# High and low part of the moving tiles as two blocks, each at its own distance from the weights

## The chip, the cores and the metric

The kernel runs on one core of one Trainium2 chip. The metric is the device time of one execution in microseconds, as the median of several runs.

## What is computed

Two layers of a hybrid trunk, run for two groups of 128 tokens each (a context group and a denoising group) that share all weights; the model is 2048 wide, the MLP 8192. Cut to what matters:

```python
def run(x, cond, s_init, latent):
    cond_act = silu(cond)
    for layer in range(2):
        sh1, sc1, g1, sh2, sc2, g2 = split(cond_act @ w_ada[layer] + b_ada[layer], 6)
        h = rms_norm(x, norm_g[layer, 0]) * (1 + sc1) + sh1
        m = hyena(h, ...) if layer == 0 else retention(h, ...)   # projections in, mixer, projection out
        x = x + g1 * m
        h = rms_norm(x, norm_g[layer, 1]) * (1 + sc2) + sh2
        x = x + g2 * (square(relu(h @ w1[layer])) @ w2[layer])
    return rms_norm(x, final_g)
```

The Hyena mixer has an input projection to 3 x 2048 and an output projection; the retention mixer has projections q and k (2048 each), v and g (4096 each) and `w_o` from 4096 back to 2048. All is float32.

## The kernel before

The activations are held transposed, features on the 128 partitions and the 256 tokens of both groups along the free axis. To reach float32 accuracy with the one-pass float32r matmul, each weight tile and each activation tile is split in a high part (the value rounded to float32r) and a low part (the rest), and a product is three matmuls: weight high by activation high (L348), weight high by activation low (L349), weight low by activation high (L350), all into one PSUM tile of 256 columns. The weight part is the operand that is loaded into the array (128 columns), the activation part is the moving one (256 columns). `gemm` (L357) runs over output tiles of 128 features and steps of 8 feature tiles, so one step is 24 matmuls; `next_w` hands it a pair `wh`, `wl` of 128 x 1024 that ScalarE (L293, high) and VectorE (L296, low) made from a weight tile that SyncE's DMA queue brought. For v and g, `gemm_v` (L428) turns the roles round: the activation part is loaded and the weight part moves, 512 columns (L440 to L442).

All instructions stand in an order written out by hand; the adaLN products are woven into it, most of them on VectorE (L254), some on TensorE (L241, groups of 16 matmul records with 256 columns), a few per stage.

Stages in order of time, with their number of 256-column matmuls and the moving tile: Hyena input projection (2304, `ht0`), Hyena output projection (768, `zt`), MLP 0 (3072 on `ht1` for w1 and 3072 on `ut` for w2, in four rounds that alternate), retention (per head 192 for q and k on `ht2`, 192 of 512 columns for v and g; 1536 and 1536 in all; 1536 on `yt` for `w_o` in four groups), MLP 1 (3072 on `ht3`, 3072 on `ut`).

Where the tiles lie: every `wh` and `wl` buffer is 4096 bytes per partition and all start at the same residue modulo 256 bytes, and a weight tile of 128 columns is 512 bytes, so every weight load starts at that one residue. `SHIFT` (L72) gives for each moving tile its distance from the weights modulo 256 bytes: 192 for all, 0 for `ht2`. A moving tile is 128 x 2 x 512 elements: for each of two feature tiles 256 high elements and then 256 low ones, 1024 bytes each, so high and low parts have the same distance. The tiles of pool `h` (`ht0` to `ht3` and part of `yt`) are 1088 elements and are used from an offset (`slid`, L83); the pools `u` (`zt`, `ut`, the rest of `yt`) begin at distance 192 (`U_BASE`). `norm_tiles` (L530) writes `ht`, `split_to` (L576) writes `ut`, `fin` (L945) `zt` and `ytr` (L1212) `yt`: each time a high part on ScalarE and a low part on VectorE. `WIDE` (L26) is empty, so what it would switch on never runs.

Of the kernel before, what the change touches and what calls it, by code (L numbers as in the profile page):

```python
# [10 lines left out]
F32 = mybir.dt.float32  # L11
# [6 lines left out]
P = 128  # L18
# [7 lines left out]
WIDE = ()  # L26
# [5 lines left out]
U_BASE = 192  # L32
# [66 lines left out]
def hybrid_trunk_kernel(ctx: ExitStack, tc, a):  # L99
# [241 lines left out]
    def products(acc, w, x, first, last):  # L341

        wh, wl = w
        if acc.shape[-1] == 512:
            T.matmul(acc, wh, x, start=first, stop=False)
            T.matmul(acc[:, 0:256], wl, x[:, 0:256], start=False, stop=last)
            return
# [9 lines left out]
    def gemm(act, n_half, evacs, mid=None, first=None, clear=None, lead=LEAD, wide=False):  # L357
# [7 lines left out]
        def open_acc(t):  # L365
            opens.setdefault(t, True)
            if first is None or t >= FIRST:
                accs[t] = pacc.tile([P, 512 if wide else 256], F32, tag="acc", name="acc")
# [146 lines left out]
    def norm_mod(l, h, pool):  # L515
# [12 lines left out]
        return (lambda k: tiles[k // 2][:, k % 2, :]), mid  # L528

    def norm_tiles(l, h, rstd, nt, seq, tiles, small=False):  # L530


        def scale(i):
            t = nt.tile([P, 2, 256], F32, tag="nt", name="nt") if small else \
                nt.tile([P, 2, 512], F32, tag="u", name="nt")[:, :, 0:256]
# [840 lines left out]
```

## Time and profile before

| | |
|---|---|
| median of 3 runs | 2872.66 us (2871.03 to 2876.06) |
| the profiled execution | 2874.03 us |
| its span, first to last instruction | 2872.3 us |
| mean granted clock of TensorE | 0.986 |
| busy: PE, PEld, DVE, ACT | 98%, 91%, 71%, 48% |
| DMA, mean | 244 GB/s |

PE is TensorE's matmul, PEld its weight load, DVE VectorE, ACT ScalarE. A matmul's shown duration (276 to 284 ns for 256 columns) is longer than the distance from one start to the next (113 to 120 ns), since matmuls are pipelined. To get that distance, starts have to be compared, or counts in a stretch of known length.

### The profile page before, as it was taken

To read this page: it belongs to the slowest core of one execution; us is meant where nothing else is said; L and a number is where in the kernel's file an instruction comes from. 1 tells how busy PE (TensorE), PEld (TensorE's weight loads), DVE (VectorE), ACT (ScalarE), POOL (GpSimd) and SP (SyncE) were. 2 spreads that over 40 slices of the span, in tenths; PEclk is the share of its full clock that TensorE was granted. 3 is DMA by queue.
4 is the path that set the end of the run, shared out by engine and by line. 5 is a ranking of instruction groups with operands and counts; after the bars stand their busy time and mean duration, and the time that the engine had idled before them with its cause. 6 is when DMAs were issued, how large, how long until landed. Compare 5 with 4: busy or idle time off the path is not lost.

```text
span 2872.3 us, 52521 instructions
## 1 busy us (share of the span) xinstructions
PE 2806.4 (98%) x22182; PEld 2625.6 (91%) x22182; DVE 2052.0 (71%) x2587; ACT 1389.9 (48%) x1960; POOL 24.7 (1%) x57
## 2 busy tenths in 40 slices
PE   7999999999999999999999999999999999999998
PEld 3689899989999999998888988988889999999998
DVE  3589999767777777786766887888774555555656
ACT  3454543465453443546545445454455445354554
POOL 1000000000000000000000000000000000000000
PEclk8999999999999999999999999999999999999999
DMA  9867776677676676666766676777665555565652
GB/s 368 322 245 282 269 286 246 246 267 273 245 265 242 244 268 241 253 242 243 251 246 224 232 278 246 256 264 281 239 234 206 201 206 200 197 224 213 224 192 103
DMA packets 105650, 701.03 MB, mean 244 GB/s; under 512 B 12115, under 2 KB 12308, under 8 KB 25796
## 3 DMA queue, kind: packets, MB, share of 16 engines
q1 hardware_dynamic: 95698, 672.58, 65.3%
q0 software_dynamic: 4384, 15.51, 1.5%
q10 hardware_dynamic: 5330, 9.57, 0.9%
q8 instruction: 174, 2.85, 0.4%
q14 instruction: 64, 0.52, 0.0%
HBM read 687.13 MB, written 10.49 MB: 243 GB/s over the span
## 4 chain that ended last, share of the span: by engine, by line
PE 86%; issue 5%; DVE 5%; DMA 3%; ACT 1%; POOL 0%; POOLq 0%; ACTq 0%; DVEq 0%
PE acc L348 23%; PE acc L349 23%; PE acc L350 23%; PE accv L440 3%; PE accv L442 3%; PE accv L441 3%; PE ada_ps L241 1%; DVE junk L254 1%; DVE wl L296 1%; DMA raw<-w_ada 1%; PE y_ps L1185 1%; ACT wh L293 1%; DMA st<-state 1%; DMA xT<-x 1%; PE y_ps L940 0%
## 5 line engine op out<-in xcount | busy, mean ns | idle before, releaser
L296 DVE TENSOR_TENSOR wl<-raw,wh 128x1024 fp32r<-128x1024 f32 x896 | 1092.6, 1224 | 666.0 <-ACT wh L293 664.6
L293 ACT CAST wh<-raw 128x1024 fp32r<-128x1024 f32 x896 | 940.2, 1053 | 1093.6 <-PE acc L349 842.6
L348 PE MATMUL acc<-ht,wh 128*128 128x256 f32 x3328 | 944.7, 284 | 6.2 <-ACT wh L293 6.2
L350 PE MATMUL acc<-ht,wl 128*128 128x256 f32 x3328 | 937.4, 282 | 6.1 <-DVE wl L296 6.1
L349 PE MATMUL acc<-ht,wh 128*128 128x256 f32 x3328 | 936.2, 281 | 0.6 <-DVE ht L560 0.6
L348 PEld LDWEIGHTS acc<-ht,wh 128*128 128x128 f32 x3328 | 634.5, 191 | 20.4 <-issue 9.4
L350 PEld LDWEIGHTS acc<-ht,wl 128*128 128x128 f32 x3328 | 636.8, 191 | 8.1 <-DVE wl L296 8.0
L349 PEld LDWEIGHTS acc<-ht,wh 128*128 128x128 f32 x3328 | 633.1, 190 | 2.8 <-issue 1.2
L348 PE MATMUL acc<-ut,wh 128*128 128x256 f32 x2048 | 572.6, 280 | 0.0
L350 PE MATMUL acc<-ut,wl 128*128 128x256 f32 x2048 | 572.5, 280 | 0.0
L349 PE MATMUL acc<-ut,wh 128*128 128x256 f32 x2048 | 572.4, 279 | 0.0
L254 DVE CUSTOM_DVE_ANT_0 junk<-raw,cb 128x2048 bf16<-128x2048 f32 x224 | 511.6, 2284 | 0.0
L350 PEld LDWEIGHTS acc<-ut,wl 128*128 128x128 f32 x2048 | 388.3, 190 | 0.1
L348 PEld LDWEIGHTS acc<-ut,wh 128*128 128x128 f32 x2048 | 386.6, 189 | 0.8 <-issue 0.8
L349 PEld LDWEIGHTS acc<-ut,wh 128*128 128x128 f32 x2048 | 384.4, 188 | 0.0
L440 PE MATMUL accv<-wh,ht 128*128 128x512 f32 x512 | 204.7, 400 | 0.0
L442 PE MATMUL accv<-wh,ht 128*128 128x512 f32 x512 | 200.1, 391 | 0.0
L441 PE MATMUL accv<-wl,ht 128*128 128x512 f32 x512 | 199.4, 389 | 0.0
L348 PE MATMUL acc<-yt,wh 128*128 128x256 f32 x512 | 143.4, 280 | 0.0
L349 PE MATMUL acc<-yt,wh 128*128 128x256 f32 x512 | 141.7, 277 | 0.0
L350 PE MATMUL acc<-yt,wl 128*128 128x256 f32 x512 | 141.6, 277 | 0.0
L440 PEld LDWEIGHTS accv<-wh,ht 128*128 128x128 f32 x512 | 96.2, 188 | 21.5 <-ACT wh L293 1.4
(213 smaller groups left out, 2480.5 us busy)
## 6 DMA issues: line engine op xcount, KB each, us to landing
raw<-w SPq DMA_DIRECT2D x250, 1024.0 KB, 5.0
raw<-w_ada SPq DMA_DIRECT2D x192, 1024.0 KB, 6.4
raw<-w_qkvg SPq DMA_DIRECT2D x93, 1024.0 KB, 5.5
raw<-hy_w_in SPq DMA_DIRECT2D x42, 1024.0 KB, 5.8
raw<-w_o SPq DMA_DIRECT2D x32, 1024.0 KB, 5.0
raw<-hy_w_out SPq DMA_DIRECT2D x12, 1024.0 KB, 6.7
st<-state POOLq DMA_DIRECT2D x16, 512.0 KB, 4.2
new_state<-so ACTq DMA_DIRECT2D x32, 256.0 KB, 4.6
```

The source lines that it names most:

```text
L241: T.matmul(st_["ps"][32 * c:32 * c + 32, :], cpad[:, 2 * u[4] + k, :], w[:, k, 256 * c:256 * c + 256], start=not started and k == 0, stop= ...
L254: V.tensor_tensor_reduce(out=junk, in0=raws[u[1:5]], in1=cb[:, r], scale=1.0, scalar=0.0, op0=ALU.mult, op1=ALU.add, accum_out=st_["acc"][ ...
L293: S.copy(whf, src)
L296: V.tensor_tensor(out=wl.rearrange("p k c -> p (k c)"), in0=src, in1=whf.bitcast(F32), op=ALU.subtract)
L348: T.matmul(acc, wh, x[:, 0:256], start=first, stop=False)
L349: T.matmul(acc, wh, x[:, 256:512], start=False, stop=False)
L350: T.matmul(acc, wl, x[:, 0:256], start=False, stop=last)
L440: T.matmul(accs[r], hi, wh[:, k, :], start=first, stop=False)
L441: T.matmul(accs[r], hi, wl[:, k, :], start=False, stop=False)
L442: T.matmul(accs[r], lo, wh[:, k, :], start=False, stop=last)
L1185: T.matmul(s["y", 1], s["qd"][:, d, q, :], s["state", d][:, q, :], start=False, stop=(d == 1 and q == 1))
```

## The change

High and low part of a moving tile become two blocks of 512 elements, one behind the other (each holding two feature tiles of 256), and the low block can be pushed away from the high one by up to 64 elements. `SHIFT` now holds a pair for each stage: the high block's distance from the weights in bytes modulo 256, and how much further the low block lies.

| tile | high, low before | high, low after |
|---|---|---|
| `ht0` | 192, 192 | 192, 224 |
| `zt` (`hy_u`) | 192, 192 | 192, 192 |
| `ht1` | 192, 192 | 192, 0 |
| `ut` in MLP 0 | 192, 192 | 96, 192 |
| `ht2` | 0, 0 | 192, 192 |
| `yt` | 192, 192 | 192, 192 |
| `ht3` | 192, 192 | 32, 64 |
| `ut` in MLP 1 | 192, 192 | 224, 224 |

`slid` returns the two blocks as a pair of access patterns; `k_of` picks feature tile k of both, and `products`, `gemm_v` and the writers take the pair in place of column ranges of one tile. The `u` tiles of the MLPs become 1088 elements (9 per pool), those of `hy_u` and `ret_u` stay at 1024. `shifted` and all that hangs on `WIDE` are removed. The diff, cut to its core:

```diff
-SHIFT = {"ht0": 192, "ht1": 192, "ht2": 0, "ht3": 192, "yt": 192, "hy_u": 192, "mlp_u0": 192, "ret_u": 192, "mlp_u1": 192}
...
-def slid(pool, name):
-
-    o = SHIFT[name] // 4
-    t = pool.tile([P, 1088], F32R, tag="h", name=name)
-    return t[:, o:o + 1024].rearrange("p (a b) -> p a b", a=2)
+SHIFT = {"ht0": (192, 32), "ht1": (192, 64), "ht2": (192, 0), "ht3": (32, 32), "yt": (192, 0),
+         "hy_u": (192, 0), "mlp_u0": (96, 96), "ret_u": (192, 0), "mlp_u1": (224, 0)}
+
+
+def slid(pool, tag, name, at, n=1088):
+
+    a, b = SHIFT[at]
+    a, b = (a - (U_BASE if tag == "u" else 0)) % 256 // 4, b // 4
+    t = pool.tile([P, n], F32R, tag=tag, name=name)
+    return tuple(t[:, o:o + 512].rearrange("p (k c) -> p k c", k=2) for o in (a, a + 512 + b))
+
+
+def k_of(tiles, k):
+    return tuple(t[:, k % 2, :] for t in tiles[k // 2])
...
         wh, wl = w
-        if acc.shape[-1] == 512:
...
-        T.matmul(acc, wh, x[:, 0:256], start=first, stop=False)
-        T.matmul(acc, wh, x[:, 256:512], start=False, stop=False)
-        T.matmul(acc, wl, x[:, 0:256], start=False, stop=last)
+        hi, lo = x
+        T.matmul(acc, wh, hi, start=first, stop=False)
+        T.matmul(acc, wh, lo, start=False, stop=False)
+        T.matmul(acc, wl, hi, start=False, stop=last)
...
-                    hi, lo = (x[:, o + r * 128:o + (r + 1) * 128] for o in (0, 256))
+                    hi, lo = (part[:, r * 128:(r + 1) * 128] for part in x)
...
-            ht = slid(hp, ("ht0", "ht1", "ht2", "ht3")[2 * l + h])
-            S.copy(ht[:, :, 0:256], slots[i][0])
+            ht = slid(hp, "h", "ht", f"ht{2 * l + h}")
+            S.copy(ht[0], slots[i][0])
...
-            V.tensor_tensor(out=ht[:, :, 256:512], in0=h32, in1=ht[:, :, 0:256].bitcast(F32), op=ALU.subtract)
+            V.tensor_tensor(out=ht[1], in0=h32, in1=ht[0].bitcast(F32), op=ALU.subtract)
...
-        S.copy(dst[:, 0:256], src)
-        return lambda: V.tensor_tensor(out=dst[:, 256:512], in0=src, in1=dst[:, 0:256].bitcast(F32), op=ALU.subtract)
+        S.copy(dst[0], src)
+        return lambda: V.tensor_tensor(out=dst[1], in0=src, in1=dst[0].bitcast(F32), op=ALU.subtract)
...
-                        us[j // 2] = up.tile([P, 2, 512], F32R, tag="u", name="ut")
+                        us[j // 2] = slid(up, "u", "ut", f"mlp_u{l}")
...
-            yt = slid(hp, "yt") if h == 7 else \
-                up.tile([P, 2, 512], F32R, tag="u", name="yt")
+            yt = slid(hp, "h", "yt", "yt") if h == 7 else slid(up, "u", "yt", "ret_u", 1024)
```

## Rows read from the trace of the kernel before

**Rows 1.** The page: engines, granted clock in 40 slices, chain that ended last.

```profile
PE 2806.4 (98%) x22182; PEld 2625.6 (91%) x22182; DVE 2052.0 (71%) x2587; ACT 1389.9 (48%) x1960; POOL 24.7 (1%) x57
...
PEclk8999999999999999999999999999999999999999
...
PE acc L348 23%; PE acc L349 23%; PE acc L350 23%; PE accv L440 3%; PE accv L442 3%; PE accv L441 3%; PE ada_ps L241 1%; DVE junk L254 1%; DVE wl L296 1%; DMA raw<-w_ada 1%; PE y_ps L1185 1%; ACT wh L293 1%; DMA st<-state 1%; DMA xT<-x 1%; PE y_ps L940 0%
```

**Rows 2.** The page, a costly group: out<-in xcount | busy us, mean ns | idle before, releaser.

```profile
L293 ACT CAST wh<-raw 128x1024 fp32r<-128x1024 f32 x896 | 940.2, 1053 | 1093.6 <-PE acc L349 842.6
```

**Rows 3.** Windows view, clean stretches of both MLPs: busy us and count of each engine.

```profile
core 0: us, PE busy (x) PEld busy (x) DVE busy (x) ACT busy (x) POOL busy (x), PEclk, DMA share, GB/s
...
640.00:680.00 40.00, 40.00 (x355) 40.00 (x355) 32.04 (x34) 23.65 (x37) 0.00 (x0) 1.00 0.76 282
...
780.00:860.00 80.00, 80.00 (x682) 80.00 (x681) 60.79 (x63) 44.98 (x70) 0.00 (x0) 1.00 0.77 281
...
2510.00:2590.00 80.00, 80.00 (x708) 80.00 (x707) 46.77 (x50) 46.83 (x72) 0.00 (x0) 1.00 0.61 212
```

**Rows 4.** Timeline of TensorE in the q/k projection: start us, us, instruction.

```profile
1613.64 0.28 PE L348 MATMUL acc<-ht,wh 128*128 128x256 f32 x1
...
1631.64 0.28 PE L348 MATMUL acc<-ht,wh 128*128 128x256 f32 x1
```

**Rows 5.** Timeline of all engines at 640 us: matmul (PE) and weight load (PEld).

```profile
640.04 0.28 PE L348 MATMUL acc<-ht,wh 128*128 128x256 f32 x1
...
640.05 0.19 PEld L349 LDWEIGHTS acc<-ht,wh 128*128 128x128 f32 x1
```

**Rows 6.** Timeline of TensorE around the ada products at 695 us.

```profile
694.10 0.28 PE L348 MATMUL acc<-ut,wh 128*128 128x256 f32 x1
...
695.01 0.28 PE L350 MATMUL acc<-ut,wl 128*128 128x256 f32 x1
...
695.22 1.07 PE L241 MATMUL ada_ps<-raw,cpad 128*32 128x256 f32 x16
...
696.44 0.28 PE L349 MATMUL acc<-ut,wh 128*128 128x256 f32 x1
...
697.85 0.28 PE L349 MATMUL acc<-ut,wh 128*128 128x256 f32 x1
```

**Rows 7.** Timeline of TensorE around the ada products at 626 us.

```profile
625.99 1.07 PE L241 MATMUL ada_ps<-raw,cpad 128*32 128x256 f32 x16
...
628.14 0.28 PE L348 MATMUL acc<-ht,wh 128*128 128x256 f32 x1
...
629.84 0.28 PE L348 MATMUL acc<-ht,wh 128*128 128x256 f32 x1
```

**Rows 8.** Lines view, L349, from 150, 478, 684 (two), 1616, 2061, 2238 (two) us.

```profile
L349 PE MATMUL acc<-ht,wh 128*128 128x256 f32 x685 | 192.4, 281 | 0.0
...
L349 PE MATMUL acc<-zt,wh 128*128 128x256 f32 x256 | 72.5, 283 | 0.3 <-DVE zt L949 0.3
...
L349 PE MATMUL acc<-ut,wh 128*128 128x256 f32 x1018 | 285.9, 281 | 0.0
...
L349 PE MATMUL acc<-ht,wh 128*128 128x256 f32 x769 | 216.1, 281 | 0.0
...
L349 PE MATMUL acc<-ht,wh 128*128 128x256 f32 x45 | 12.7, 283 | 0.0
...
L349 PE MATMUL acc<-yt,wh 128*128 128x256 f32 x203 | 56.0, 276 | 0.0
...
L349 PE MATMUL acc<-ut,wh 128*128 128x256 f32 x429 | 120.5, 281 | 0.0
...
L349 PE MATMUL acc<-ht,wh 128*128 128x256 f32 x257 | 72.2, 281 | 0.0
```

**Rows 9.** Timeline of TensorE in the v and g projections.

```profile
1528.07 0.39 PE L440 MATMUL accv<-wh,ht 128*128 128x512 f32 x1
...
1530.79 0.39 PE L440 MATMUL accv<-wh,ht 128*128 128x512 f32 x1
```

More of the change, by code (lines that the diff above doesn't have):

```diff
@@ L25 @@
 OLEAD = 4
-WIDE = ()
 SKIP = 4
@@ L31 @@
 SCRATCH = 2048
-U_BASE = 192
 NACC = 4
@@ L355, in next_w, with gemm @@
         return ready.popleft()[1:]
-    def gemm(act, n_half, evacs, mid=None, first=None, clear=None, lead=LEAD, wide=False):
+    def gemm(act, n_half, evacs, mid=None, first=None, clear=None, lead=LEAD):
         accs, opens = {}, {}
@@ L367, in open_acc @@
             if first is None or t >= FIRST:
-                accs[t] = pacc.tile([P, 512 if wide else 256], F32, tag="acc", name="acc")
+                accs[t] = pacc.tile([P, 256], F32, tag="acc", name="acc")
             elif t < FIRST // 2:
@@ L527, in mid @@
             norm_tiles(l, h, rstd, pool, NORM_SEQ[1], tiles)
-        return (lambda k: tiles[k // 2][:, k % 2, :]), mid
+        return (lambda k: k_of(tiles, k)), mid
     def norm_tiles(l, h, rstd, nt, seq, tiles, small=False):
@@ L534, in scale @@
             t = nt.tile([P, 2, 256], F32, tag="nt", name="nt") if small else \
-                nt.tile([P, 2, 512], F32, tag="u", name="nt")[:, :, 0:256]
+                nt.tile([P, 1024 if (l, h) == (1, 0) else 1088], F32, tag="u",
+                        name="nt")[:, 0:512].rearrange("p (k c) -> p k c", k=2)
             V.tensor_tensor(out=t, in0=xT[i], in1=rstd.unsqueeze(1).broadcast_to([P, 2, 256]), op=ALU.mult)
@@ L945, in fin @@
             def fin():
[L946 removed]
+                z = slid(up, "u", "zt", "hy_u", 1024)
                 src = st["src"].rearrange("p i r t -> p i (r t)")
[L948 to L949 removed]
+                S.copy(z[0], src)
+                V.tensor_tensor(out=z[1], in0=src, in1=z[0].bitcast(F32), op=ALU.subtract)
                 zt[b] = z
@@ L984, in mlp @@
                 us = {}
-                wide = l in WIDE
-                def both(out, acc):
-                    S.copy(out, acc[:, 256:512])
-                    V.tensor_tensor(out=out, in0=out, in1=acc[:, 0:256], op=ALU.add)
                 def evac(j, acc):
                     if j // 2 not in us:
-                        us[j // 2] = up.tile([P, 2, 512], F32R, tag="u", name="ut")
+                        us[j // 2] = slid(up, "u", "ut", f"mlp_u{l}")
                     r = ms.tile([P, 256], F32, tag="r", name="r")
-                    def square_of(s):
-                        S.activation(out=r, in_=s, func=AF.Relu)
-                        u = ms.tile([P, 256], F32, tag="uu", name="uu")
-                        S.activation(out=u, in_=r, func=AF.Square)
-                        return split_to(us[j // 2][:, j % 2], u)
-                    if not wide:
-                        return square_of(acc)
-                    both(r, acc)
-                    return lambda: square_of(r)
+                    S.activation(out=r, in_=acc, func=AF.Relu)
+                    u = ms.tile([P, 256], F32, tag="uu", name="uu")
+                    S.activation(out=u, in_=r, func=AF.Square)
+                    return split_to(k_of(us, j), u)
                 def evac2(j, acc):
@@ L1009, in evac2 @@
                     if q == 0:
-                        both(m, acc) if wide else S.copy(m, acc)
+                        S.copy(m, acc)
                     else:
-                        for o in range(0, acc.shape[-1], 256):
-                            V.tensor_tensor(out=m, in0=m, in1=acc[:, o:o + 256], op=ALU.add)
+                        V.tensor_tensor(out=m, in0=m, in1=acc, op=ALU.add)
                     if q == 3:
@@ L1021, in evac2 @@
                         return norm_in
-                gemm(act, 2, [lambda acc, j=j: evac(j, acc) for j in range(16)], mid, wide=wide)
+                gemm(act, 2, [lambda acc, j=j: evac(j, acc) for j in range(16)], mid)
                 mid = None
-                gemm(lambda k: us[k // 2][:, k % 2, :], 2, [lambda acc, j=j: evac2(j, acc) for j in range(16)], wide=wide)
+                gemm(lambda k: k_of(us, k), 2, [lambda acc, j=j: evac2(j, acc) for j in range(16)])
                 flush(True)
@@ L1232, in yact @@
                     run_one()
-                return yts[4 * g + k // 2][:, k % 2, :]
+                return k_of({i: yts[4 * g + i] for i in (k // 2,)}, k)
             gemm(yact, 1, [lambda acc, j=j: residual(1, 2, j, acc, g == 3) for j in range(16)])
```

26 lines of the change are left out of this document (8 added, 18 removed).

## Prediction

> **What bounds the kernel now.** I read the page first. TensorE is busy for 98% of the span, at a granted clock of full speed in all but the first slices, and three quarters of the chain that ended last are the matmuls of L348 to L350 and L440 to L442 [rows 1]. The time therefore goes where the start-to-start distance of the matmuls goes, and nothing the change touches runs anywhere else. ScalarE's weight casts spend more time waiting for a matmul than working [rows 2], so the producers have slack. The bulk is 18,432 matmuls with 256 moving columns (L348 to L350): 2304 in the Hyena input projection, 768 in its output projection, 3072 on `ht` and 3072 on `ut` in each MLP, 1536 for q and k, 1536 for `w_o`. Beside them stand 1536 with 512 moving columns for v and g (L440 to L442).
>
> Next I compared clean stretches by the windows view. A window's count holds about two matmuls that only overlap an edge, so I take two off. From 2510 to 2590 us there are 708, so 80/706 = 113.3 ns each; from 780 to 860 there are 682, so 80/680 = 117.6 ns; clock 1.00 and PE without a gap in both [rows 3]. Two MLP stretches with the same instructions, shapes and addresses modulo 256 thus run at two levels. The third level is the q/k projection, the one stage at distance 0: from 1613.64 to 1631.64 us lie 150 matmuls, 18.00/150 = 120.0 ns [rows 4]. I call them fast, slow and colliding. The mean duration marks the level too: 276, 281 and 283 ns [rows 8]. Weights for the next matmul are loaded while the current one streams: the load of 640.05 starts 0.01 us after the matmul of 640.04 [rows 5]. So two reads of SBUF run side by side, and their relative address (0 against 192) has a price of 120.0 - 113.3 = 6.7 ns, or 2.4 ns against the slow level.
>
> What flips fast and slow is an interruption. Before the ada products at 695.22 us 8 steps from 694.10 to 695.01 are 0.114 us each, after them 12 steps from 696.44 to 697.85 are 0.1175 [rows 6]; the same kind of interruption at 625.99 ends in the fast level, 15 steps from 628.14 to 629.84 at 0.113 [rows 7]. Nothing resets the level until the next interruption, so MLP 0 stays slow from 696 to 1316 us and MLP 1 from 2238 to 2480 [rows 8], and the stretch behind that is fast [rows 3].
>
> **What sits above the fast level now**, per stage, as count times price. Input and output projection: means of 281 and 283 with waits in them [rows 8]; as a mix of levels I put 3 ns on each, 2304 x 3 = 7 us and 768 x 3 = 2.3. MLP 0: 1018 + 769 triples after 684 us at 281 [rows 8], 5361 x 4.3 = 23. q/k: 1536 x 6.7 = 10. `w_o`: 276 in its last part [rows 8], 1 for the rest. MLP 1: 429 + 257 triples at 281 from 2238 on [rows 8], 2058 x 4.3 = 9; behind them it is fast [rows 3]. Together 52 us, 1.8% of the span.
>
> **The change, part by part.** *Instructions.* None is added, removed or reordered; WIDE was empty, so its removal takes out code that never ran. The writers of the moving tiles now write two contiguous blocks where they wrote interleaved halves: same element counts, and they wait for TensorE anyway [rows 2]. Price 0. If that cover went, a writer's own extra time would have to reach TensorE; I find no row that makes it more than zero. `u` tiles of the MLPs grow by 256 bytes, so what follows them moves by whole multiples of 256 and keeps its residue. *Distances* (high, low part): `ht0` 192, 224; `ht1` 192, 0; `ht2` 192, 192; `ht3` 32, 64; `ut` of MLP 0 96, 192; `ut` of MLP 1 224, 224; `zt` and `yt` stay at 192, 192.
>
> *q/k*, 0 to 192: the nearest rows are the ones at 192, fast or slow [rows 3], so 113.3 to 117.6 instead of 120.0. Interruptions every few steps draw both; I take the middle, 115.5, which gives 1536 x 4.5 = 7 us. *v and g*: here `ht2` is the loaded operand and the distance of the moving weights from it goes from 0 to 64 (256 - 192). Now 12 matmuls take 2.72 us from 1528.07 to 1530.79, 226.7 ns [rows 9], exactly twice the fast level, so distance 0 costs nothing visible here. Distance 64 is in no row. Bounds: one load of 128 columns per matmul can cost or give back the colliding price, 6.7 ns either way, x 1536 = 10 us slower or faster. I take 0, the nearest row, and keep both ends.
>
> *MLPs and input projection*, untested distances: of the 14,592 matmuls there, 9984 get a residue that no 256-column row shows or that only q/k shows (768 low parts of `ht0`, 1024 of `ht1`, all 3072 of `ht3`, 2048 high parts of the first `ut`, all 3072 of the second). Bounds by the nearest rows: 113.3 to 120.0. I take 114.3 as mean of these stages, a quarter of the way from fast to slow. The reason: the fast level is reachable after interruptions at 192 [rows 7], and the slow level needs the same relation in all three matmuls of a triple to hold for hundreds of microseconds; a low block at another distance than the high block changes the relation twice per triple, which should throw the two reads out of the slow relation as an interruption does. That part is inference, not a row. Sum: MLP 0 23 - 6144 x 1.0 ns = 17 us gained; MLP 1 9 - 6 = 3; input projection 7 - 2.3 = 4.7, of which I count 3, since VectorE products for adaLN stand in the chain, 1% of the span [rows 1]. *Output projection, `w_o`:* unchanged.
>
> Total 7 + 0 + 17 + 3 + 3 = 30 us. The profiled execution took 2874.0 (span 2872.3 and 1.7 around it), 1.4 above the median of 2872.7; its time less 30 is 2844, and the median's equivalent is **2843 us**. What is late next: nothing new; at the fast level of 640 to 680 us DMA is at 0.76 and VectorE at 32 of 40 us with PE gapless [rows 3], in the stage with the most ada work.
>
> **Rivals.** *A redraw.* The distances only re-roll which level each interruption ends in, half and half. Then 18,432 x 2.15 = 40 us stay above fast instead of 52: 2872.7 - 12 = 2861, with a swing of 13 us for each MLP, since one draw holds for a whole MLP [rows 8]. For it: two draws at one distance [rows 6, 7]. Against: nothing but that q/k never draws fast at 0.
>
> *New collisions (slower).* The untested residues 224, 32, 64 and 96 behave as 0 does. Place: L348 to L350 in the input projection and both MLPs; price 6.7 ns over fast for each of 9984 matmuls, 67 us; the rest at 192 keep 19 us (8448 x 2.2). That is 86 against 52: 2907. It decides from (52 - 19)/6.7 ns = 4900 colliding matmuls on. For it: `ht1`'s low part goes to 0, the one residue known to collide [rows 4]. Against: the other 8960 are at residues whose only known neighbour, 192, can run free.
>
> *The change does nothing.* The levels come from the interruptions alone. Time 2873. What speaks for it is that one address runs at two levels [rows 3]; against it, that 150 matmuls in a row stay at 120.0 at distance 0 [rows 4]. The Trainium skill would have it so: "SBUF — State Buffer", section "A bandwidth-pool intuition that's wrong (but worth ruling out)", gives TensorE a second, independent read port for its weight loads and calls SBUF's macros multi-ported, so a load's address should not matter to the streaming read. The trace disagrees, 120.0 [rows 4] against 113.3 and 117.6 [rows 3], and the measurement decides; I leave the rule a small chance.
>
> *Below fast.* 256 columns at one per 2.4 GHz cycle would be 106.7 ns; no 256-column stretch here shows less than 113.3. If the two MLPs came halfway, to 110, that would be 12,288 x 4.3 = 53 us below the forecast: 2790.
>
> **How the numbers follow.** Forecast 0.58 (its own range 2821, all 52 us gone, to 2862); redraw 0.20, of which 0.13 faster, 0.04 within, 0.03 slower; collisions 0.12; nothing 0.06; below fast 0.04. A measurement of this kernel tells about 0.2% from no change, 5.7 us. Faster 0.58 + 0.13 + 0.04 = 0.75; same 0.04 + 0.06 = 0.10; slower 0.03 + 0.12 = 0.15. The range leaves out most of the collisions and of below fast: 2812 (all gone and v and g at their lower bound) to 2878 (a redraw with both MLPs mostly slow).
>
> **What would show it.** Right: q/k durations drop from 283 to 276 or 281; in MLP 0 the count in 80 us rises from 682 towards 706, and the same in MLP 1 before 2480 us; the interruption near 695 us no longer raises the spacing. Wrong: any stage at 283 (a collision: look first at `ht1` in MLP 0, whose low part is at 0), v and g above 227 ns, or MLPs still split between 276 and 281 with the flips at ada products. A gap of PE with a writer of `ut` or `ht` as releaser would show that the block writes matter after all.

## The result: slower, at one level from end to end

The changed kernel takes 2892.35 us (median of 3 runs, 2890.18 to 2894.82) against 2872.66 us before: a ratio of 1.0067 with an interval of [1.0044, 1.009]. The forecast was 2843 us with a range up to 2878, so both the sign and the range were wrong. The profiled execution took 2894.82 us, its span is 2893.1 us, 20.8 us longer than before. The lines of the change have moved: L348, L349, L350 are now L343, L344, L345; L440 to L442 are L435 to L437; L293 is L292; the ada products of L241 are at L240.

The page of the changed kernel, engines and chain by line, to be laid beside [rows 1]:

```profile
PE 2829.5 (98%) x22182; PEld 2646.2 (91%) x22182; DVE 2051.1 (71%) x2587; ACT 1386.7 (48%) x1960; POOL 24.6 (1%) x57
...
PE acc L343 23%; PE acc L344 23%; PE acc L345 23%; PE accv L437 3%; PE accv L436 3%; PE accv L435 3%; DVE junk L253 2%; DVE wl L295 2%; PE ada_ps L240 1%; DMA raw<-w_ada 1%; PE y_ps L1168 1%; ACT wh L292 1%; DMA st<-state 1%; DMA xT<-x 0%; PE y_ps L936 0%
```

Counts and the engines' shares are the same, VectorE and ScalarE within 3.2 us of their old busy time; TensorE alone is busy 23.1 us longer, 2.3 more than the span grew. So no new wait came in: the same matmuls stand further apart.

Where they do is read from the tile view, which gives the first and the last start of a tile's matmuls. Kernel before: first matmul on `ht1`, last on the first `ut`, last on `yt`, last on the second `ut`:

```profile
L348 PE MATMUL acc<-ht,wh x256: 276/276/580, 588.5 to 683.9; 128*128 128x256 f32 x128
...
L350 PE MATMUL acc<-ut,wl x1024: 276/281/388, 684.5 to 1318.2; 128*128 128x256 f32 x171
...
L350 PE MATMUL acc<-yt,wl x512: 276/276/288, 1566.3 to 2131.8; 128*128 128x256 f32 x171
...
L350 PE MATMUL acc<-ut,wl x2048: 276/281/388, 684.5 to 2857.6; 128*128 128x256 f32 x187
```

The same four of the changed kernel:

```profile
L343 PE MATMUL acc<-ht,wh x256: 279/281/415, 589.2 to 685.9; 128*128 128x256 f32 x128
...
L345 PE MATMUL acc<-ut,wl x1024: 278/279/303, 686.5 to 1326.2; 128*128 128x256 f32 x171
...
L345 PE MATMUL acc<-yt,wl x512: 276/276/288, 1574.4 to 2136.5; 128*128 128x256 f32 x171
...
L345 PE MATMUL acc<-ut,wl x2048: 277/279/303, 686.5 to 2878.7; 128*128 128x256 f32 x187
```

Up to `ht1` the two differ by 0.7 us (589.2 against 588.5). MLP 0 takes 737.0 us (589.2 to 1326.2) where it took 729.7: +7.3. Retention takes 810.3 where it took 813.6: -3.3. MLP 1 takes 742.2 where it took 725.8: +16.4. With the 0.7 us ahead of them that is +21.1 us: the loss lies in the MLPs, in the second more than in the first.

Windows of 80 us in the MLPs of the changed kernel, columns as in [rows 3]; the fourth and fifth columns are busy us and count of PE and PEld. In order: `ht1`, first `ut`, then in MLP 1 `ut`, `ht3`, `ht3`, `ut`:

```profile
780.00:860.00 80.00, 80.00 (x673) 80.00 (x672) 60.12 (x62) 44.06 (x69) 0.00 (x0) 1.00 0.72 266
875.00:955.00 80.00, 80.00 (x677) 80.00 (x676) 60.53 (x64) 29.40 (x28) 0.00 (x0) 1.00 0.73 265
2250.00:2330.00 80.00, 80.00 (x679) 80.00 (x678) 40.66 (x35) 33.49 (x43) 0.00 (x0) 1.00 0.58 209
2340.00:2420.00 80.00, 80.00 (x682) 80.00 (x681) 43.66 (x47) 45.68 (x73) 0.00 (x0) 1.00 0.60 213
2520.00:2600.00 80.00, 80.00 (x681) 80.00 (x681) 43.75 (x47) 45.01 (x71) 0.00 (x0) 1.00 0.61 214
2610.00:2690.00 80.00, 80.00 (x678) 80.00 (x678) 44.66 (x49) 29.96 (x29) 0.00 (x0) 1.00 0.63 225
```

As in the prediction two matmuls of each count only overlap an edge. So `ht1` stands at 80/671 = 119.2 ns, the first `ut` at 118.5, `ht3` at 117.6 to 117.8 and the second `ut` at 118.2 to 118.3, all at full clock and with PE gapless. Before, MLP 0 stood at 117.6 in this stretch and MLP 1 behind 2482 us at 113.3 [rows 3]. No stretch of either MLP in the changed kernel stands at 113.3.

The timeline of TensorE in the changed kernel, three places. Around the ada products at 697.72 us:

```profile
694.08 0.28 PE L343 MATMUL acc<-ut,wh 128*128 128x256 f32 x1
...
697.28 0.28 PE L343 MATMUL acc<-ut,wh 128*128 128x256 f32 x1
...
697.72 1.07 PE L240 MATMUL ada_ps<-raw,cpad 128*32 128x256 f32 x16
...
699.19 0.28 PE L343 MATMUL acc<-ut,wh 128*128 128x256 f32 x1
...
701.67 0.28 PE L343 MATMUL acc<-ut,wh 128*128 128x256 f32 x1
```

27 steps ahead of it take 3.20 us, 118.5 ns, and 21 behind it 2.48 us, 118.1 ns: the interruption that moved the level from 114 to 117.5 before [rows 6] moves nothing now. In the q/k projection:

```profile
1620.89 0.28 PE L343 MATMUL acc<-ht,wh 128*128 128x256 f32 x1
...
1640.04 0.28 PE L344 MATMUL acc<-ht,wh 128*128 128x256 f32 x1
```

169 steps in 19.15 us, 113.3 ns, where it was 120.0 [rows 4]. And v and g:

```profile
1523.16 0.39 PE L435 MATMUL accv<-wh,ht 128*128 128x512 f32 x1
...
1530.72 0.39 PE L435 MATMUL accv<-wh,ht 128*128 128x512 f32 x1
```

33 steps in 7.56 us, 229.1 ns, where 226.7 stood in [rows 9]. That row was the faster of two kinds: by the starts, v and g of the kernel before run at 226.7 in some parts of each stretch and at 228.8 in others, and the eight stretches take 408.9 us before and 410.5 after.

So each stage of the MLPs has become steady, at a level between 117.6 and 119.2 ns, and the question is why the fast level is gone.

### The profile page after: what moved, and what is told of

Its sections match the earlier page's. It is cut to its first block, busy times and chain, and to the rows that moved or that the text cites. A ratio compares the mean times of both kernels' runs of the same rounds, so it can differ in the third digit from the quotient of the medians.

```text
span 2893.1 us, 52521 instructions
## 1 busy us (share of the span) xinstructions
PE 2829.5 (98%) x22182; PEld 2646.2 (91%) x22182; DVE 2051.1 (71%) x2587; ACT 1386.7 (48%) x1960; POOL 24.6 (1%) x57
## 4 chain that ended last, share of the span: by engine, by line
PE 84%; DVE 6%; issue 5%; DMA 3%; ACT 1%; POOL 0%; POOLq 0%; ACTq 0%; DVEq 0%
PE acc L343 23%; PE acc L344 23%; PE acc L345 23%; PE accv L437 3%; PE accv L436 3%; PE accv L435 3%; DVE junk L253 2%; DVE wl L295 2%; PE ada_ps L240 1%; DMA raw<-w_ada 1%; PE y_ps L1168 1%; ACT wh L292 1%; DMA st<-state 1%; DMA xT<-x 0%; PE y_ps L936 0%
## 5 line engine op out<-in xcount | busy, mean ns | idle before, releaser
L292 ACT CAST wh<-raw 128x1024 fp32r<-128x1024 f32 x896 | 937.9, 1050 | 1117.9 <-PE acc L344 878.5
L343 PE MATMUL acc<-ht,wh 128*128 128x256 f32 x3328 | 947.5, 285 | 5.6 <-ACT wh L292 5.6
L345 PE MATMUL acc<-ht,wl 128*128 128x256 f32 x3328 | 936.2, 281 | 6.2 <-DVE wl L295 6.2
L344 PE MATMUL acc<-ht,wh 128*128 128x256 f32 x3328 | 939.2, 282 | 0.5 <-DVE ht L556 0.5
L343 PEld LDWEIGHTS acc<-ht,wh 128*128 128x128 f32 x3328 | 631.1, 190 | 20.3 <-ACT wh L292 7.8
L345 PEld LDWEIGHTS acc<-ht,wl 128*128 128x128 f32 x3328 | 631.7, 190 | 7.9 <-DVE wl L295 7.9
L344 PEld LDWEIGHTS acc<-ht,wh 128*128 128x128 f32 x3328 | 632.0, 190 | 2.8 <-issue 1.2
L344 PE MATMUL acc<-ut,wh 128*128 128x256 f32 x2048 | 578.4, 282 | 0.0
L343 PE MATMUL acc<-ut,wh 128*128 128x256 f32 x2048 | 575.0, 281 | 0.0
L345 PE MATMUL acc<-ut,wl 128*128 128x256 f32 x2048 | 574.8, 281 | 0.0
L345 PEld LDWEIGHTS acc<-ut,wl 128*128 128x128 f32 x2048 | 387.1, 189 | 0.0
L343 PEld LDWEIGHTS acc<-ut,wh 128*128 128x128 f32 x2048 | 385.1, 188 | 0.8 <-issue 0.8
L344 PEld LDWEIGHTS acc<-ut,wh 128*128 128x128 f32 x2048 | 385.2, 188 | 0.0
L435 PE MATMUL accv<-wh,ht 128*128 128x512 f32 x512 | 204.1, 399 | 0.0
L437 PE MATMUL accv<-wh,ht 128*128 128x512 f32 x512 | 201.1, 393 | 0.0
L343 PE MATMUL acc<-yt,wh 128*128 128x256 f32 x512 | 143.4, 280 | 0.0
L344 PE MATMUL acc<-yt,wh 128*128 128x256 f32 x512 | 141.6, 277 | 0.0
L345 PE MATMUL acc<-yt,wl 128*128 128x256 f32 x512 | 141.6, 277 | 0.0
L435 PEld LDWEIGHTS accv<-wh,ht 128*128 128x128 f32 x512 | 96.2, 188 | 22.6 <-ACT wh L292 1.7
```

What stands on the lines that cost most here:

```text
L292: S.copy(whf, src)
L343: T.matmul(acc, wh, hi, start=first, stop=False)
L344: T.matmul(acc, wh, lo, start=False, stop=False)
L345: T.matmul(acc, wl, hi, start=False, stop=last)
L435: T.matmul(accs[r], hi, wh[:, k, :], start=first, stop=False)
L437: T.matmul(accs[r], lo, wh[:, k, :], start=False, stop=last)
```

## Experiments

All edits are to the changed kernel; "192 throughout" is `all_192`, the kernel from which most of the later ones differ by one thing. Ratios are to the kernel before, run beside each on the same chip. There its median was 2852 to 2859 us, with single runs from 2844 to 2887. Its 2872.66 us of the first comparison lies in the upper part of that, which is told again below.

### The layout alone, and 192 throughout

`layout_only` gives both blocks the distances of before, `all_192` the same with q/k at 192.

```diff
-SHIFT = {"ht0": (192, 32), "ht1": (192, 64), "ht2": (192, 0), "ht3": (32, 32), "yt": (192, 0),
-         "hy_u": (192, 0), "mlp_u0": (96, 96), "ret_u": (192, 0), "mlp_u1": (224, 0)}
+SHIFT = {"ht0": (192, 0), "ht1": (192, 0), "ht2": (0, 0), "ht3": (192, 0), "yt": (192, 0),
+         "hy_u": (192, 0), "mlp_u0": (192, 0), "ret_u": (192, 0), "mlp_u1": (192, 0)}
```

> The changed kernel with the old distances put back (192 for both blocks everywhere, 0 for ht2); the block layout, the larger ut tiles and the removed code stay. Theory (the distances cost the 20 us): as the kernel before, 2873 within 10, MLP levels of 113.3 and 117.6 ns both present, q/k at 120. Rival (the block layout or the larger tiles cost it): as the changed kernel, 2892, with MLP 1 nowhere at 113.3.

> The changed kernel with 192 for both blocks in every stage, ht2 too, so of the change only the layout and ht2's new distance are left. Theory: q/k falls from 120.0 to about 114 ns, 1536 x 6 = 9 us less, v and g rise from 227.8 to 229.0, 2 us more, so 7 us under the kernel before, 2866, if the MLPs draw the same levels as there. Rival (every change of a stage's timing draws the later levels anew): the MLPs run at other levels than in the kernel before, and the time lies anywhere from 2845 to 2890.

`layout_only`: 2851.99 us, ratio 1.0014 [0.9992, 1.0037]. `all_192`: 2846.59 us (2838.68 to 2869.56), ratio 0.9999 [0.9968, 1.003]. Windows of `layout_only` in MLP 0, in MLP 1 ahead of the ada products, and behind them:

```profile
780.00:860.00 80.00, 80.00 (x709) 80.00 (x707) 63.50 (x64) 47.09 (x75) 0.00 (x0) 1.00 0.79 290
2210.00:2300.00 90.00, 90.00 (x797) 90.00 (x796) 48.07 (x43) 41.47 (x55) 0.00 (x0) 1.00 0.58 201
2490.00:2570.00 80.00, 80.00 (x681) 80.00 (x681) 44.06 (x47) 46.04 (x73) 0.00 (x0) 1.00 0.62 215
```

113.2, 113.2 and 117.8 ns: the two levels of before are back, only that here MLP 0 drew the fast one and the end of MLP 1 the slow one, the other way round from [rows 3]. So the blocks, the writers and the larger `u` tiles cost nothing that shows; the distances do. Both kernels came out some 20 us under the times expected, and so did the kernel before beside them (2852.40 us), so the ratios decide. Which level a stage gets seems to be drawn anew in each run ("drawn" is meant in that sense from here on): the ten runs of `all_192` spread over 31 us.

### Which distances can run fast

Two kernels with high and low part at one distance per stage.

```diff
+# survey_a: "ht0": (64, 0),  "ht1": (32, 0),  "mlp_u0": (64, 0), "ht3": (96, 0),  "mlp_u1": (128, 0)
+# survey_b: "ht0": (160, 0), "ht1": (160, 0), "mlp_u0": (0, 0),  "ht3": (224, 0), "mlp_u1": (32, 0)
```

> One distance for both blocks in each stage, another one per stage: ht0 64, ht1 32, ut of MLP 0 64, ht3 96, ut of MLP 1 128; ht2, zt, yt at 192. Theory (only 192 can run free): each of these stages holds one level between 117 and 121 ns from end to end, and the time is 2890 to 2910. Rival (what costs is that the two blocks differ): stages with equal distances draw between 113.3 and a slow level as at 192.

> As the run before with ht0 160, ht1 160, ut of MLP 0 at 0, ht3 224, ut of MLP 1 32. Theory (only 192 can run free): one level between 117 and 121 ns in each, 120.0 in ut of MLP 0 as in q/k of the kernel before. Rival (what costs is that the two blocks differ): levels of 113.3 appear at 160, 224 or 32.

2895.32 and 2893.50 us, one run each. Windows of `survey_a`: `ht1` at 32 (first and second round that are clean), `ut` at 64 between them, then `ut` at 128 and `ht3` at 96:

```profile
788.00:868.00 80.00, 80.00 (x669) 80.00 (x669) 59.92 (x61) 44.29 (x71) 0.00 (x0) 1.00 0.75 275
880.00:960.00 80.00, 80.00 (x708) 80.00 (x707) 63.48 (x67) 30.83 (x30) 0.00 (x0) 1.00 0.78 280
968.00:1048.00 80.00, 80.00 (x688) 80.00 (x687) 61.88 (x66) 45.44 (x71) 0.00 (x0) 1.00 0.73 263
2240.00:2320.00 80.00, 80.00 (x676) 80.00 (x675) 38.90 (x33) 33.41 (x43) 0.00 (x0) 1.00 0.61 211
2332.00:2412.00 80.00, 80.00 (x669) 80.00 (x668) 42.97 (x45) 44.22 (x71) 0.00 (x0) 1.00 0.61 211
```

And of `survey_b`: `ht1` at 160, `ut` at 0, `ut` at 32, `ht3` at 224:

```profile
786.00:866.00 80.00, 80.00 (x684) 80.00 (x683) 61.06 (x63) 44.90 (x70) 0.00 (x0) 1.00 0.76 280
876.00:956.00 80.00, 80.00 (x669) 80.00 (x669) 59.54 (x64) 28.69 (x29) 0.00 (x0) 1.00 0.74 262
2250.00:2330.00 80.00, 80.00 (x688) 80.00 (x687) 40.46 (x35) 33.42 (x43) 0.00 (x0) 1.00 0.63 219
2340.00:2420.00 80.00, 80.00 (x679) 80.00 (x677) 43.39 (x47) 44.95 (x70) 0.00 (x0) 1.00 0.60 215
```

In ns per matmul: 0 119.9; 32 116.6 (and 119.9 in one round); 64 113.3 (and, by starts, 117.8 in its first round); 96 119.9; 128 118.7; 160 117.3; 192 113.3 or 117.8 (above); 224 118.2. A theory by which 192 alone can run fast falls with the 113.3 at 64. These two lie 128 apart, and the other distances come in pairs 128 apart too that are close: 0 and 128, 32 and 160, 96 and 224 differ by 0.7 to 1.7 ns. Of the eight, only 64 and 192 showed the fast level; 32 has two levels as well, 116.6 and 119.9, both above it. The second `ut` of the changed kernel, (224, 224), stands at 118.2 to 118.3, which is what 224 costs by itself.

### Two good distances mixed, and the changed kernel again

```diff
+# pair_64_192: "ht0", "ht1", "ht3", "mlp_u0", "mlp_u1": (64, 128)   -> high 64, low 192
+# after_again: no edit
```

> High block at 64, low block at 192 in the input projection and both MLPs; the rest at 192. Both residues have shown a fast level of 113.3 to 113.5 ns. Theory (two differing distances take the fast level away): one level of 117 to 119 ns from end to end in these stages, 2880 to 2895. Rival (what costs in the change is the residue each block was given; differing blocks break the slow relation, as the prediction had it): 113.3 in both MLPs from end to end, 2820 to 2835.

> The changed kernel once more, beside runs of the kernel before on the same chip. Theory (its pairs leave no fast level to draw, the kernel before draws): its runs lie close together near 2892, those of the kernel before spread over 2843 to 2876, and the ratio is 1.005 to 1.017 depending on these draws. Rival (the changed kernel draws too): its runs spread as widely as those of the kernel before.

`pair_64_192`: 2889.06 us, ratio 1.0087 [1.0055, 1.0118]. Windows in `ht1`, `ut` of MLP 0 and `ht3`:

```profile
786.00:866.00 80.00, 80.00 (x681) 80.00 (x681) 60.03 (x62) 45.56 (x71) 0.00 (x0) 1.00 0.74 276
878.00:958.00 80.00, 80.00 (x681) 80.00 (x680) 61.03 (x66) 29.51 (x28) 0.00 (x0) 1.00 0.74 266
...
2518.00:2598.00 80.00, 80.00 (x682) 80.00 (x681) 43.79 (x46) 44.91 (x70) 0.00 (x0) 1.00 0.62 216
```

117.6 to 117.8 ns, in both MLPs from end to end. Each of the two distances reaches 113.3 alone; alternating within a triple (the three matmuls of one product: high, low, high) they do in no stretch of this profile. As both reach 113.3 alone, this is the run that shows the price of the difference by itself. `after_again` took 2894.98 us with a spread of 3.3 us over 4 runs, ratio 1.0107 [1.0058, 1.0157], where the kernel before spread over 30 us beside it. So the changed kernel has hardly any draws left, and the size of the loss against before depends on what before happens to draw: 0.7% against the three runs of the first comparison, 1.1% here.

### What draws the level, and whether the address matters

`fill8` is 192 throughout with the ada products that TensorE did inside the MLPs moved ahead of each MLP; `moved_32` puts 32 bytes ahead of all tiles, so that all tiles move and the distances stay.

```diff
+# fill8, on all_192
-FILL = 6
+FILL = 8
+# moved_32, on all_192: the first tile of the first pool, ahead of the weights
+    per.tile([P, 8], F32, name="pad")
```

> 192 everywhere, and FILL 8 for 6: the two groups of ada products that lay inside each MLP on TensorE stand at the stage's start. Theory (an interruption of TensorE is what draws the level): each MLP holds one level, fast or slow, from about 40 us after its start to its end, with no flip at the places near 692 and 2450 us of the run with 192 everywhere. Rival (levels flip by themselves or by traffic): flips inside the MLPs as before.

> 192 everywhere, and 32 bytes put ahead of the first tile, so that weights and moving tiles all lie 32 bytes further: distances as before, residues of the addresses themselves changed (the weights begin at 0 modulo 256 instead of 224). Theory (the distance counts): the levels are 113.3 and 117.6 to 117.8 as before, 2838 to 2876. Rival (the address itself counts): other levels, below 113 or near 120.

`fill8`: 2910.36 us. Both MLPs hold one level without a flip, but it is the slow one: windows of 80 us at 790, 880, 2265 and 2450 us count 681, 681, 681 and 682, 117.6 to 117.8 ns. (Its time is no measure of the levels, since the products it moves leave TensorE waiting elsewhere: 10.9 us for their weights at 580 to 593 us.) The timeline of `fill8` ahead of MLP 0 shows where the level was drawn:

```profile
619.04 0.28 PE L344 MATMUL acc<-ht,wh 128*128 128x256 f32 x1
...
623.12 0.28 PE L344 MATMUL acc<-ht,wh 128*128 128x256 f32 x1
...
624.71 0.28 PE L344 MATMUL acc<-ht,wh 128*128 128x256 f32 x1
...
630.36 0.28 PE L344 MATMUL acc<-ht,wh 128*128 128x256 f32 x1
```

36 steps at 113.3 ns, then 12 in 1.59 us instead of 1.36, in which TensorE paused twice for some 0.1 us each, then 48 steps at 117.7. No ada product is there: a short pause can draw too. In the MLPs of the profiles at 192 throughout, each change of level stands at a pause of TensorE. What made these two pauses is open. `moved_32`: 2850.01 us; windows at 780, 2220 and 2490 us count 708, 682 and 708, so 113.3, 117.6 and 113.3 ns as at the old address. So the distance counts, and the place shows no effect, in one run.

### One tile out of step

If a change of distance throws the two reads out of the slow level, a single one per pass should do. `kick_ut` is 192 throughout with the first of the eight moving tiles of each pass over `ut` at 160; `kick_all` does so in `ht0`, `ht1` and `ht3` as well; `kick_lo` moves only the low block of that tile.

```diff
-def slid(pool, tag, name, at, n=1088):
+def slid(pool, tag, name, at, n=1088, kick=0):
...
-    a, b = SHIFT[at]
+    a, b = SHIFT[at][0] - kick, SHIFT[at][1]             # kick_ut, kick_all
+    a, b = SHIFT[at][0], (SHIFT[at][1] - kick) % 256     # kick_lo
...
-                        us[j // 2] = slid(up, "u", "ut", f"mlp_u{l}")
+                        us[j // 2] = slid(up, "u", "ut", f"mlp_u{l}", kick=32 if j < 2 else 0)
...
+            ht = slid(hp, "h", "ht", f"ht{2 * l + h}", kick=32 if i == 0 and (l, h) != (1, 0) else 0)   # kick_all only
```

> All stages at one distance, 192, except the first of the eight moving tiles of each of the two MLP passes, which lies at distance 160: 6 of every 48 matmuls of a pass at another distance. In the survey every block that came to distance 64 from 32 ran at 113.5 ns, and 160 to 192 is the same step. Theory that such a step throws the pair of reads out of the slow level: both MLPs near 113.3 ns for seven eighths and 117 to 120 for one eighth, some 114 ns, with no long slow stretch, and 2826 to 2840 us with a spread of under 15 us between runs. Rival, that a level is kept only where every matmul has the same distance (as with 64 and 192 mixed): both MLPs at 117 to 118 throughout, 2870 to 2895 us. Third, that the step does nothing: levels of 113.3 and 117.8 in long stretches as with 192 alone, 2840 to 2875 us, spread over 20 us.

> As kick_ut, with the first tile of each of the three input projections at 160 as well. The step theory: input projections at 114 to 115 ns too, and 2815 to 2830 us. The rival: they run at 117 to 118 as well, 2875 to 2900 us. If the step does nothing: as with 192 alone, 2840 to 2875 us.

> As kick_ut, but of the first of the eight moving tiles of each MLP pass over ut only the low block lies at 160; its high block stays at 192: 2 of 48 matmuls of a pass, each alone between matmuls at 192, in place of 6 in a row. If one matmul at another distance is enough to throw the reads out of the slow level: ut near 113.3 ns from end to end, with under a nanosecond on the passes, and 2835 to 2843 us. If a run of several is needed: levels of 113.3 and 117.8 in long stretches as with 192 alone, 2838 to 2875 us with a spread over 20. If an alternating distance is itself what holds the slow level (as with 64 and 192 mixed): ut at 117 to 118 throughout, 2865 to 2885 us.

`kick_ut`: 2844.46 us (2838.11 to 2851.71), ratio 0.9934 [0.99, 0.9969], faster than before and, by the ratios, some 1.7% faster than the changed kernel. `kick_all`: 2847.45 us, 0.994 [0.9906, 0.9973]. `kick_lo`: 2845.64 us (2839.12 to 2861.0), 0.9973 [0.9948, 0.9997]. Windows of `kick_ut` on `ht1` and `ut`:

```profile
780.00:860.00 80.00, 80.00 (x708) 80.00 (x708) 62.96 (x64) 47.09 (x74) 0.00 (x0) 1.00 0.79 289
865.00:945.00 80.00, 80.00 (x704) 80.00 (x703) 63.35 (x65) 31.74 (x33) 0.00 (x0) 1.00 0.75 265
```

And of `kick_lo` on `ut`:

```profile
862.00:942.00 80.00, 80.00 (x705) 80.00 (x704) 63.68 (x66) 30.92 (x30) 0.00 (x0) 1.00 0.75 273
```

`ut` stands at 114.0 and 113.8 ns, `ht1` behind it at 113.3, and behind 735 us no slow stretch of more than some 20 us is left on `ut` in the profiles of all three. Only the first `ht` round of an MLP, ahead of which no tile is out of step, still draws: by its starts it stood at 117.8 ns from 2179 to 2213 us in `kick_ut`. The theory that such a step (a change of distance from one matmul to the next) ends a slow stretch holds, but not at the first tile each time. In the profile of `kick_lo` the stretches that were slow up to 700.9 and 2213.6 us are fast behind the low blocks there. In that of `kick_ut` one stretch stays slow longer:

```profile
2452.30 0.28 PE L343 MATMUL acc<-ut,wh 128*128 128x256 f32 x1
...
2468.91 0.28 PE L343 MATMUL acc<-ut,wh 128*128 128x256 f32 x1
```

141 steps in 16.61 us, 117.8 ns, almost three passes of 48, so two kicked tiles went by without ending it; behind the next it is fast. `kick_ut` and `kick_lo` came out 3 to 4 us above what was expected, and `kick_all` some 17 above: on `ht1` its window counts 703 where that of `kick_ut` counts 708, 114.1 against 113.3 ns, and its Hyena input projection, which waits for weights and is interrupted every few steps, is only 1.7 us shorter. `kick_lo` has two runs near 2860, so that one low block does it every time isn't shown; the tile of `kick_ut` left a spread of 14 us. One sentence of the expectation of `kick_ut` was wrong: of the blocks that came to 64 from 32 in `survey_a`, the first (from 692.5 us) ran at 117.8 and not at 113.5.

The rule that a stage at mixed distances stays slow, and this one, look opposed: one differing low block brings the fast level, one in every triple keeps the spacing near 118. Both follow if the step itself has a price. In `kick_lo` a pass of 48 matmuls has two triples with a differing low block and takes, by the starts of whole rounds, 113.89 ns on the mean: 27 ns more than one at 113.33, 13.3 ns for each such triple (13.6 in the expectations that follow). By starts the slow level costs 3 x (117.78 - 113.33) = 13.3 ns a triple: the same. So the runs don't tell a price of the step from a triple that runs at the slow level for its own length. And 4.0 of the 13.3 ns are what a matmul at 160 costs by itself in `survey_b` (117.3).

### The price of a step, by dose

`lo_half` moves the low block of every second tile, `lo_all` that of all.

```diff
-                        us[j // 2] = slid(up, "u", "ut", f"mlp_u{l}", kick=32 if j < 2 else 0)
+                        us[j // 2] = slid(up, "u", "ut", f"mlp_u{l}", kick=32 if j % 4 < 2 else 0)   # lo_half
+                        us[j // 2] = slid(up, "u", "ut", f"mlp_u{l}", kick=32)                       # lo_all
```

> As kick_lo, but the low block of every second of the eight moving tiles of a pass over ut lies at 160: 24 of the 48 matmuls stand in a triple whose low block differs. From kick_lo a triple of hi, hi, lo with a differing low block took some 13.6 ns more than the 340 ns of three at the fast level, and the matmuls after it went on at 113.3. Theory, that each such triple costs this much by itself and nothing else: ut at (340 + 13.6 / 2) / 3 = 115.6 ns on the mean of a pass from end to end, the ht half near 113.3, and 2842 to 2858 us. Rival, that a low block which differs often enough brings back the slow level: ut at 117 to 118 throughout.

> As kick_lo, but the low blocks of all tiles of ut lie at 160, so that every triple differs, as in the changed kernel. Theory, that the step is paid once per triple: (340 + 13.6) / 3 = 117.9 ns from end to end of ut, never 113.3, and 2855 to 2875 us. Rival, that the levels near 118 of the changed kernel belong to its own distances, 96 and 224, and not to the step: 192 with 160 then runs in levels with 113.3 among them.

`lo_half`: 2850.21 us, ratio 0.9986 [0.9959, 1.0012]. `lo_all`: 2863.99 us, 1.0026 [0.9981, 1.0072]. `lo_half` on `ut`, then `ht1`:

```profile
864.00:944.00 80.00, 80.00 (x694) 80.00 (x694) 62.53 (x66) 30.16 (x29) 0.00 (x0) 1.00 0.76 271
952.00:1032.00 80.00, 80.00 (x708) 80.00 (x708) 64.13 (x69) 46.76 (x72) 0.00 (x0) 1.00 0.73 263
```

`lo_all`, the same two:

```profile
867.00:947.00 80.00, 80.00 (x681) 80.00 (x681) 61.06 (x64) 30.22 (x29) 0.00 (x0) 1.00 0.74 265
957.00:1037.00 80.00, 80.00 (x708) 80.00 (x708) 64.13 (x69) 46.89 (x72) 0.00 (x0) 1.00 0.72 263
```

With 2, 8 and 16 differing triples out of 16 in a pass (one eighth, half, all), `ut` stands at 113.8, 115.6 and 117.8 ns; by a price of 13.6 ns a triple it should be 113.9, 115.6 and 117.9. And `ht1`, all at 192, runs at 113.3 behind each. The price is paid for each triple whose parts differ, and what follows runs fast.

### Whose loss it is

The changed kernel with the MLPs' `ut` put back to 192, and with the three `ht` stages put back.

```diff
+# after_mlp192
-         "hy_u": (192, 0), "mlp_u0": (96, 96), "ret_u": (192, 0), "mlp_u1": (224, 0)}
+         "hy_u": (192, 0), "mlp_u0": (192, 0), "ret_u": (192, 0), "mlp_u1": (192, 0)}
+# after_in192
-SHIFT = {"ht0": (192, 32), "ht1": (192, 64), "ht2": (192, 0), "ht3": (32, 32), "yt": (192, 0),
+SHIFT = {"ht0": (192, 0), "ht1": (192, 0), "ht2": (192, 0), "ht3": (192, 0), "yt": (192, 0),
```

> The changed kernel with the two MLPs alone put back to distance 192 for both blocks; the other stages keep the new pairs. Theory, that the pairs of the MLPs took away the fast level there: the MLPs run at 113.3 and 117.8 in long stretches again, the time falls by 10 to 45 us from that of the changed kernel, to 2848 to 2883, and the spread between runs grows from some 4 to over 15 us; the input projections stay at 118 to 119. Rival, that the loss lies in the input projections and the projections behind them: the time stays within 5 us of 2893.

> The changed kernel with the three stages ht0, ht1 and ht3 put back to distance 192 for both blocks; the MLPs' ut keeps the new pairs (96, 192) and (224, 224). Theory, that each stage's loss is its own: ut stays at 118.5 and 118.2 ns; ht0 falls from 118.8 to a mix near 116.8, ht1 and ht3 run at 113.3 or 117.8 in place of 119.0 and 117.9; the time lies between 2849 and 2885 us. With the 25 us of the run with ut put back, the two shares then add up to the difference to the kernel with 192 throughout, some 48 us. Rival, that the level of one stage is carried into the next, so that nothing is won until both are put back: ht1 and ht3 stay above 117.5 throughout, and the time is above 2880 us.

`after_mlp192`: 2868.28 us, ratio 1.0024 [0.999, 1.0058]. `after_in192`: 2873.09 us, 1.0054 [1.0035, 1.0073]. `after_mlp192`, `ht1`, `ut` and `ht3`:

```profile
780.00:860.00 80.00, 80.00 (x673) 80.00 (x672) 59.76 (x62) 44.92 (x70) 0.00 (x0) 1.00 0.76 276
870.00:950.00 80.00, 80.00 (x709) 80.00 (x708) 63.56 (x66) 31.57 (x30) 0.00 (x0) 1.00 0.77 276
2320.00:2400.00 80.00, 80.00 (x682) 80.00 (x681) 43.48 (x47) 45.05 (x71) 0.00 (x0) 1.00 0.62 217
```

`after_in192`, `ht1`, `ut`, `ut` of MLP 1 and `ht3`:

```profile
780.00:860.00 80.00, 80.00 (x709) 80.00 (x708) 63.76 (x66) 47.10 (x74) 0.00 (x0) 1.00 0.79 289
868.00:948.00 80.00, 80.00 (x677) 80.00 (x676) 60.56 (x64) 29.40 (x28) 0.00 (x0) 1.00 0.74 265
2232.00:2312.00 80.00, 80.00 (x679) 80.00 (x678) 39.97 (x33) 33.70 (x43) 0.00 (x0) 1.00 0.60 212
2500.00:2580.00 80.00, 80.00 (x682) 80.00 (x681) 43.79 (x46) 44.83 (x70) 0.00 (x0) 1.00 0.61 216
```

Each stage has its loss for itself: the part that was not put back keeps its 119.2 and 117.6, or 118.5 and 118.2, and the part that was put back runs at 113.2 in `ut` and `ht1`. Behind a stage whose parts differ one at 192 starts fast (`ut` in `after_mlp192`, `ht1` in `after_in192`), while 192 throughout has to draw. `ht3` in `after_in192`, behind a `ut` at (224, 224) without a step, shows both levels, 117.6 in the last window and 113.3 at 2321 to 2401 us (a count of 708). Against 1.0107 of `after_again`, `ut` is worth 0.8% (24 us) and the `ht` stages 0.5% (15 us); 192 throughout is worth 1.1%. Within the intervals the parts add up to the whole.

## Why the prediction was wrong, point by point

- **What bounds it.** Right. In the windows of the MLPs TensorE is gapless before and after, and the loss is spacing.
- **No cost for the layout and its writers.** None shows: 1.0014 [0.9992, 1.0037] with the old distances.
- **q/k.** Right in kind and nearly in size. Undisturbed it runs at 113.3 ns in place of 120.0, and on the mean of all steps without a pause at 114.1 in place of 119.8. The eight stretches take 201.8 us where they took 207.4, by their first and last starts: 5.6 us gained where 7 was put, as the pauses between grew by some 3 us.
- **v and g.** 1.6 us more (410.5 against 408.9), within the bounds of 10 and not the 0 that was taken; [rows 9] shows the faster of the two kinds of stretch at distance 0. With q/k that is -4.0 us; retention came to -3.3, as it began 0.8 us later behind MLP 0.
- **MLPs and input projection at 114.3 ns: the step that failed.** It rested on one sentence, marked as an inference: a low block at another distance "should throw the two reads out of the slow relation as an interruption does". `kick_lo` shows that it does. What the step put at nothing is what such a block costs: 13.3 ns a triple at 192 with 160 and, by the 117.6 to 117.8 of `pair_64_192`, as much at 64 with 192, paid in every triple of a stage whose parts differ. That is what the slow level costs, so a stage that steps in every triple gains nothing from it. And it took distances that no row showed to be near the fast level, which is the next point. The term was 1.0 ns above the fast level; in the MLPs it measured 4.3 to 5.9. For MLP 0 the sum then has 6144 x 5.5 = 34 us above fast where 23 stood before and 6 were expected, for MLP 1 6144 x 4.7 = 29 where 9 stood before: +11 and +20 worked out, +7.3 and +16.4 read from the tile views. The sums of before count only what lies behind 684 and 2238 us; by all starts of both profiles spacing costs 8.5 and 18.3 us more, and the pauses are 1.3 and 1.4 us shorter. The input projection, where 3 us were to be gained, takes 2.5 us more from its first start to its last (101.7 to 481.1 us against 101.3 to 478.2).
- **The residues: the larger half of that step.** For the 9984 matmuls at new distances the bounds of 113.3 to 120.0 held for the mean of each stage, but a quarter of the way up was too low. Two of the eight distances reach 113.3, six stand at 116.6 to 119.9 ([rows 3, 4] show one of either kind). The second `ut` has no step at all and stands at 224's own 118.2. An estimate of the share: if each matmul paid only what its own distance cost in the survey, the MLPs would stand 1024 x 6.6 (`ht1`) + 2048 x 6.6 (first `ut`) + 2048 x 3.3 (`ht3`) + 3072 x 4.9 (second `ut`) = 42 us above fast, of the 34 + 29 = 63 that stand there. So some two thirds go to the distances themselves, and most of the rest to `ht1` and `ht3`, whose parts differ: 119.2 and 117.7 where their distances alone give 115.5 and 115.5.
- **What before was.** The 52 us above fast were those of one execution, whose MLP 0 had drawn slow. The profiles of `layout_only` and `all_192` drew it fast. The prediction's 17 us in MLP 0 were thus partly a gain over a draw, not over the kernel; with the draws of the other runs even a perfect MLP 0 would have gained less, and the loss measured is up to 1.1%.
- **The rivals.** The collisions had the right sign and the right place, the input projection and both MLPs, and 2907 us was nearer than the forecast. Its mechanism was the larger part of it: 224, 96, 32 and 0 do cost by themselves, but the pair of 64 and 192 is slow by the step alone, and `ht1` and `ht3` for the most part, which no rival named. The redraw described the kernel before well and the changed one hardly, since its MLPs draw nothing. That distances do nothing falls by the survey: 113.3 to 119.9 ns with the same instructions. There the Trainium skill's independent read port for weight loads ("SBUF — State Buffer", section "A bandwidth-pool intuition that's wrong (but worth ruling out)") does not describe what the runs show.
- **The range.** It ended at 2878, where "a redraw with both MLPs mostly slow" was the worst case counted in. The bound of the unknown distances, 120.0, was priced in the collision rival alone and left outside at 0.12; as the bound of an unmeasured term it belonged inside: 9984 x 6.7 = 67 us.

Open: what in the chip makes two levels at one distance, whether it is one of the two reads that waits, and why 64 and 192 alone run free. For pairs with a distance that costs by itself the price of the step and that of the distance don't simply add, so the shares above are rough: (32, 64) stands at 117.8, though 32 alone has 116.6 and a step would add 4.4; (96, 192) stands at 118.5, only 0.8 above what its distances alone give.

## What to carry to other kernels

When a forecast rests on a change that breaks up a bad pattern, ask what the break itself costs and how often it is paid: the kernel that pays it once per pass is 0.7% faster than the kernel before (`kick_ut`); once per triple it cost as much as it removed (`lo_all`). And a value that no row shows is not near the best one because its neighbour is: six of eight distances were not. Before a gain is counted against a profile, see from the spread of the runs whether the stretch that looks improvable is the kernel or one draw of it. A kernel whose matmuls are back to back can still gain or lose some 5% of a stage by where the moving tile lies relative to the weights, so place both at a distance that has been seen to run fast, and count matmuls in clean windows to see it.

## What the runs showed of the hardware

- With 256 moving columns of float32r, full clock and no gap, the spacing depends on the distance of the moving tile from the weights modulo 256 bytes: 113.3 ns at best (64 and 192), up to 119.9 (0 and 96). Distances 128 apart are alike within 1.7 ns, but for a round at 32 that stood at 119.9 where 160 has 117.3. Moving everything by 32 bytes changed none of the levels.
- At 64 and 192 there are two levels, 113.3 and 117.8 ns. At 192 a run kept one for hundreds of microseconds until TensorE paused, by as little as some 0.1 us twice, or until a block at another distance came by: at the first one in `kick_lo`, at the second or third in places of `kick_ut`.
- A triple whose low block lies at another distance (192 with 160, 64 with 192) costs some 13.3 ns more than 340, in proportion to the number of such triples: 113.8, 115.6 and 117.8 ns at an eighth, a half and all. A triple at the slow level takes the same 353.3 ns.
- Where the moving operand is the weight with 512 columns, distance 0 gives the lower spacing, 226.7 ns in part of its stretches and 228.8 in the rest, against 229 throughout at 64 (1.6 us in 1536 matmuls), while with 256 columns 0 is among the dearest.
